# Two merge gates of a two-layer diffusion trunk as seven block products of summed operands

## The chip, the cores and the metric

One core of one Trainium2 chip runs the whole kernel. The metric is the device time of one execution in microseconds; the time before is the median of three runs.

## What is computed

Two layers work on 512 latent and 256 context positions of 1024 channels. A layer normalises and modulates its input to h, projects h to four mixers (A: dense attention, D: windowed attention with a sink, B: FNet mixing, C: gMLP gating), gates each mixer's output and merges the four:

```python
def _merge(h, outs, gates, w_br, w_merge, b_merge, w_out):
    yb = jnp.stack([o * jax.nn.silu(z) for o, z in zip(outs, gates)], axis=2)
    y = jnp.einsum('bnrw,rwd->bnrd', yb, w_br)
    g = jax.nn.sigmoid(h @ w_merge + b_merge).reshape(b, n, N_BRANCH, D_MODEL)
    return jnp.sum(g * y, axis=2) @ w_out
...
sh, sc, gt = _modulation(c, w_ada, b_ada)       # silu(c) @ w_ada + b_ada
h = _rms(x, norm_w) * (1.0 + sc[:, None, :]) + sh[:, None, :]
x = x + gt[:, None, :] * y
```

For every mixer r, h @ w_merge is a product of 768 x 1024 by 1024 x 1024 in layer 0 (latent and context together) and of 512 x 1024 in layer 1 (latent alone).

## The kernel before, in words

Activations lie channels first: a tile is 128 channels by 768 positions, columns 0 to 255 the context (NC), 256 to 767 the latents. h is eight such tiles, each as a rounded high part hh and a remainder hl; a weight tile (128 by 512, four 128 x 128 blocks) is likewise split into wh and wl, so that every product is three matmuls: wh with hh, wh with hl, wl with hh (mm3, lines 183 to 189; mmp, 191 to 197, runs over the blocks of a piece).

Weights come as a list of pieces in the order of use (`plan`, 138 to 153). wnext (175) takes the next one: it issues loads on SP's queue up to LOADS = 5 pieces ahead into three buffers (wload, line 161) and splits pieces up to two ahead of the one in use (wround: ScalarE casts wh on line 171, VectorE subtracts wl on line 172; three buffers each).

merge(r) (649 to 689) makes one mixer's share of the merged sum M. It loops over eight output tiles j: 8 blocks of 128 input channels by 3 matmuls, each for the 512 latent columns (bank gl) and the 256 context columns (gc); then the branch, 2 blocks by 3 matmuls for both widths (yl, and the other half of gc); then ScalarE's tanh of the gate (672), VectorE's product with the branch (674), and the sum into M, by a GpSimd DMA that adds (680), or on VectorE in the last pass (678), which also splits M into MH and ML (686, 687) for the output projection outp (964).

Layer 0 goes through it in this order: R_C, then R_A inside the filler, then R_D, then R_B. The attention generator (608 to 643: scores, maximum 577, exponential 585, transposes 601, products with v 634; one score bank, `s`) is driven against a filler of projections and merges (935): after each step the filler is advanced until its cost in ns has made up the pace, 4500 in layer 0 and 4000 in layer 1 (drive, 871). What the filler has left runs after the attention. R_D and R_B then run with a side generator under SIDE = 0.42: first fnet (785, the FNet's transforms, matmuls included, whose result is R_B's operand), then ada_rest (250): the column sums that make the remaining modulation rows, 24 rows of 128 in layer 0 (48 half rows by two vectors, c and c_ctx) and 8 in layer 1 (16 half rows, c alone). A half row is loaded on SP's queue (273) into one of three buffers it shares with the attention and multiplied and summed by VectorE (276). The costs and paces only set the order in which the program is written; a scheduler then orders each engine's instructions by that order and by when it reckons them ready and their buffers free.

Rope.finish (475) rotates q and k with tables cos and sin that are loaded once (408) and kept.

## Time and profile before

| | us |
|---|---|
| three runs | 1198.5, 1201.61, 1201.41 |
| their median | 1201.41 |
| the profiled execution | 1199.38 |
| its span, first to last instruction | 1197.5 |
| TensorE busy | 1176.4 (98%) |
| its weight loads | 1000.6 (84%) |
| VectorE busy | 734.6 (61%) |
| ScalarE busy | 471.9 (39%) |
| GpSimd busy | 14.4 (1%) |

The times of the profile are counted from the first instruction, so that its own execution is 1.9 us longer than its span. The granted clock of TensorE is 1.00 in every window. A busy share counts an instruction from its start to its end; the start of one matmul to the start of the next is shorter than a matmul's own duration, since they overlap, so the cost of a run of matmuls is read from starts.

### The profile page before, as it was taken

How to read it: one execution, taken by the hardware profiler on the slowest of the kernel's cores; microseconds unless marked ns; L12 is line 12 of the kernel's file. 1: busy time of each engine (PE TensorE's matmuls, PEld its weight loads, DVE VectorE, ACT ScalarE, POOL GpSimd, SP SyncE). 2: the span in 40 equal slices, each digit the busy share in tenths (PEclk: the TensorE clock that was granted, in tenths of full speed). 3: DMA queues.
4: the chain of work that ended last, by engine and by line, in shares of the span. 5: the costliest groups of instructions: out<-in, count | busy, mean ns of one | idle time of the engine just before them, and what ended most of it. 6: DMA issues, size and time to landing. Idle time of an engine off the chain costs nothing.

```text
span 1197.5 us, 18872 instructions
## 1 busy us (share of the span) xinstructions
PE 1176.4 (98%) x7164; PEld 1000.6 (84%) x7164; DVE 734.6 (61%) x1568; ACT 471.9 (39%) x935; POOL 14.4 (1%) x20
## 2 busy tenths in 40 slices
PE   6999999999999999999999999999999999999998
PEld 3789888888888888988888888887888888888887
DVE  5683567555555553577885468768656666476543
ACT  5443634333333332422333246545444343333431
POOL 0000000000000000000000000000000000000000
PEclk9999999999999999999999999999999999999999
DMA  8718114111112335567653454462322223355353
GB/s 305 247 34 203 55 38 104 49 45 49 54 49 54 75 84 121 128 182 201 183 167 103 132 166 139 136 178 81 100 67 75 63 65 91 99 169 155 97 171 124
DMA packets 76090, 138.81 MB, mean 116 GB/s; under 512 B 9056, under 2 KB 19424, under 8 KB 76000
## 3 DMA queue, kind: packets, MB, share of 16 engines
q1 hardware_dynamic: 66640, 120.30, 34.3%
q10 hardware_dynamic: 7056, 11.02, 3.1%
q0 software_dynamic: 2304, 6.29, 3.0%
q8 instruction: 56, 0.92, 0.3%
q14 instruction: 34, 0.28, 0.1%
HBM read 115.56 MB, written 4.19 MB: 100 GB/s over the span
## 4 chain that ended last, share of the span: by engine, by line
PE 93%; DMA 2%; DVE 2%; SPq 1%; ACT 1%; issue 0%; ACTq 0%
PE gl L186 10%; PE gl L187 10%; PE gl L189 10%; PE o L634 4%; PE tp L601 3%; PE gc L186 3%; PE gc L189 3%; PE gc L187 3%; PE ow L186 3%; PE ow L189 3%; PE ow L187 3%; PE p L186 3%; PE p L189 3%; PE p L187 3%; PE yl L186 2%; PE yl L187 2%
## 5 line engine op out<-in xcount | busy, mean ns | idle before, releaser
L171 ACT CAST wh<-wr 128x512 fp32r<-128x512 f32 (+1 forms) x320 | 184.6, 577 | 369.9 <-PE gc L187 95.7
L172 DVE TENSOR_TENSOR wl<-wr,wh 128x512 fp32r<-128x512 f32 (+1 forms) x320 | 203.2, 636 | 189.0 <-ACT wh L171 187.0
L186 PE MATMUL gl<-hh,wh 128*128 128x512 f32 x512 | 204.6, 400 | 0.0
L187 PE MATMUL gl<-hl,wh 128*128 128x512 f32 x512 | 200.5, 392 | 0.0
L189 PE MATMUL gl<-hh,wl 128*128 128x512 f32 x512 | 200.3, 391 | 0.0
L189 PEld LDWEIGHTS gl<-hh,wl 128*128 128x128 f32 x512 | 96.2, 188 | 20.8
L186 PEld LDWEIGHTS gl<-hh,wh 128*128 128x128 f32 x512 | 96.6, 189 | 16.6 <-ACT wh L171 0.2
L187 PEld LDWEIGHTS gl<-hl,wh 128*128 128x128 f32 x512 | 96.7, 189 | 16.2
L577 DVE TENSOR_REDUCE mx<-s 128x1 f32<-128x768 f32 (+3 forms) x80 | 61.6, 770 | 78.2 <-PE s L571 35.8
L585 ACT ACTIVATE p<-s,ng 128x768 f32<-128x768 f32 (+3 forms) x80 | 60.1, 751 | 102.6 <-DVE ng L582 58.5
L276 DVE CUSTOM_DVE_ANT_0 aj<-at,cb 128x512 f32<-128x512 f32 x112 | 72.7, 687 | 10.6 <-DMA at<-in_wadat_dram 10.6
L186 PE MATMUL gc<-hh,wh 128*128 128x256 f32 x256 | 73.6, 288 | 0.0
L189 PE MATMUL gc<-hh,wl 128*128 128x256 f32 x256 | 72.6, 283 | 0.0
L187 PE MATMUL gc<-hl,wh 128*128 128x256 f32 x256 | 72.5, 283 | 0.0
L186 PE MATMUL p<-hh,wh 128*128 128x512 f32 (+1 forms) x192 | 71.3, 371 | 0.0
L186 PE MATMUL ow<-MH,wh 128*128 128x512 f32 (+1 forms) x200 | 69.6, 348 | 1.0 <-DVE xn L976 1.0
L189 PE MATMUL ow<-MH,wl 128*128 128x512 f32 (+1 forms) x200 | 69.5, 348 | 0.8 <-DVE wl L172 0.8
L187 PE MATMUL ow<-ML,wh 128*128 128x512 f32 (+1 forms) x200 | 69.5, 348 | 0.0
L189 PE MATMUL p<-hh,wl 128*128 128x512 f32 (+1 forms) x192 | 68.3, 356 | 0.0
L187 PE MATMUL p<-hl,wh 128*128 128x512 f32 (+1 forms) x192 | 68.2, 355 | 0.0
L672 ACT ACTIVATE g<-gl,bmh 128x512 f32<-128x512 f32 x64 | 43.9, 686 | 56.2 <-PE gl L189 39.0
L601 PE MATMUL tp<-kconst,p 128*128 128x128 f32 x368 | 53.3, 273 | 0.0
(467 smaller groups left out, 2425.3 us busy)
## 6 DMA issues: line engine op xcount, KB each, us to landing
wr<-in_wm_dram SPq DMA_DIRECT2D x128, 256.0 KB, 2.7
wr<-in_win_dram SPq DMA_DIRECT2D x72, 256.0 KB, 2.8
at<-in_wadat_dram SPq DMA_DIRECT2D x64, 256.0 KB, 3.1
wr<-in_wo_dram SPq DMA_DIRECT2D x40, 256.0 KB, 2.9
aw<-in_wada_dram SPq DMA_DIRECT2D x16, 512.0 KB, 5.9
wr<-in_wm_dram SPq DMA_DIRECT2D x64, 128.0 KB, 2.2
ks<-yk SPq DMA_DIRECT2D x32, 192.0 KB, 4.2
M<-g POOLq DMA_DIRECT2D x16, 384.0 KB, 4.6
```

What stands on the lines that cost most here:

```text
L171: A.copy(hi[:, :n], raw[:, :n])
L172: V.tensor_sub(lo[:, :n], raw[:, :n], hi[:, :n].bitcast(F32))
L186: T.matmul(d, wh, xh[:, c0:c1], start=first and op, stop=False)
L187: T.matmul(d, wh, xl[:, c0:c1], start=False, stop=False)
L189: T.matmul(d, wl, xh[:, c0:c1], start=False, stop=last and cl)
L276: V.tensor_tensor_reduce(out=junk[:, :512], in0=w[:, :512], in1=cb[2 * v + half][:, :512], scale=0.5, scalar=0.0, op0=ALU.mult, op1=ALU.ad ...
L577: V.reduce_max(out=mx, in_=sv, axis=AX.X)
L585: A.activation(p[:, :nk], sv, AF.Exp, bias=ng, scale=0.125, accum_out=sm_)
L601: T.transpose(tp[:, (i - g0) * P:(i - g0 + 1) * P], p[:, i * P:(i + 1) * P], ident)
L634: T.matmul(dst[64 * hx:64 * hx + 64, :], vt[kt_ // 3][:, kt_ % 3, c0:c0 + 64], pts[hx][:, j * P:(j + 1) * P], start=(j == 0), stop=(j == l ...
L672: A.activation(g[:, q0:q1], gp, AF.Tanh, scale=0.5, bias=bmh[:, r * 8 + j:r * 8 + j + 1])
```

## The change

In layer 0 the gates of R_D and R_B are made by merge_s, for pairs of output tiles (j, j+4). The input channels are halved (tiles 0 to 3, 4 to 7), the positions are halved (H1 = 0 to 383, H2 = 384 to 767) and the outputs are halved (j, j+4), and the eight products of blocks become seven, of summed operands: combos sums the blocks of h once for both passes (into tiles T2, T3, T4 and T1; first_sum writes T1 over the right half of hh and hl 0 to 3), and a `prep` of four VectorE instructions a pair sums the weight tiles in place, ahead of the third block. A product is 4 blocks of channels by 3 matmuls of 384 columns. Bank z holds the first product, is copied out by ScalarE, and goes on accumulating; x and y hold two more, which VectorE adds to the copies. Four weight tiles of a pair come through the pool z, two rows of branch weights as before.

R_A's last three tiles (part 5 to 7) are held back from the filler, and the FNet and combos stand beside them; PACE of layer 0 is 3900 in place of 4500. ada_rest now goes through all half rows of the first half, then the second, with one row buffer of its own (the next load is written behind the sums of the last) and two buffers for c's rows, which it shares with the rotary tables; those are loaded anew for each use, on ScalarE's queue. Its steps are laced into R_C, z1, the FNet's projection and R_A, one for each 4800 of their cost, in both layers, and in layer 0 into R_D and R_B, one for each 6500. Layer 1's R_D and R_B keep the old form.

```diff
-PACE = (4500, 4000)
+PACE = (3900, 4000)
 STK = 1000
 WHOLE = 4
 LOADS, W_RAW, W_HI, W_LO = 5, 3, 3, 3
 SIDE = 0.42
+ADA, ADA_S = 4800, 6500
+HELD = 5
...
+        def merged_s(l, r):
+            def a(j, h):
+                return (wm[l, r, j, :, 512 * h:512 * h + 512], 512, "wraw" if h and j < 4 else "z")
+            def y(j):
+                return (wm[l, r, j, :, 1024:], 256)
+            first = [load(*a(0, 0)), load(*a(4, 0)), load(*a(4, 1)), load(*a(0, 1))]
...
+                def prep(a11=a11, a12=a12, a21=a21, a22=a22, s1=s1):
+                    t = tl("p", f"s1_{a11}")[:, :512]
+                    V.tensor_add(t, raws[a21], raws[a22])
+                    V.tensor_sub(raws[a21], raws[a11], raws[a21])
+                    V.tensor_sub(raws[a11], t, raws[a11])
+                    V.tensor_sub(raws[a12], raws[a12], raws[a11])
+                    s1.append(t)
+                item(a11, 512)
+                item(a12, 512)
+                item(a12, 512, prep, lambda k=a11: raws[k])
+                item(a12, 512, None, lambda k=a21: raws[k])
+                item(a12, 512, None, lambda s1=s1: s1[0])
+                item(y0, 256)
+                item(y0, 512, None, lambda k=a12: raws[k])
+                item(y0, 512, None, lambda k=a22: raws[k])
+                item(y1, 256)
...
+                src, n, tag = loads[k]
+                if tag == "z":
+                    raws[k] = tl("z", f"wr{k}")[:, :512]
+                else:
+                    raws[k] = pw.tile([P, 512], F32, name=f"wr{k}", tag="wraw", bufs=W_RAW)
+                nc.sync.dma_start(raws[k][:, :n], src)
...
+            wload(max(k for k, *_ in items[i:i + LOADS]))
+            wround(i + 2)
+            while prepped[0] < min(i + 3, len(items)):
+                prep = items[prepped[0]][2]
+                if prep:
+                    prep()
+                prepped[0] += 1
...
+            steps = [(half, l, j) for half in range(2) for l, j in names]
+            macc = {g: pc.tile([P, 8 if g else 16, 2, 2], F32, name=f"macc{g}{nv}", tag=f"macc{g}")
+                    for g in sorted({j // 16 for _, j in names})}
+            row, cb = [], []
+            def fetch(i):
+                if i < len(steps):
+                    half, l, j = steps[i]
+                    w = prow.tile([P, 512], F32, name=f"at{l}_{j}_{half}{nv}", tag="row")
+                    nc.sync.dma_start(w, wadat[l, j, :, half * 512:half * 512 + 512])
+                    row.append(w)
+            fetch(0)
...
+                for v in range(nv):
+                    junk = tl("sc", f"aj{l}_{j}_{half}{v}")
+                    V.tensor_tensor_reduce(
+                        out=junk[:, :512], in0=row[i], in1=cb[v], scale=0.5,
+                        scalar=0.0, op0=ALU.mult, op1=ALU.add, accum_out=macc[j // 16][:, j % 16, v, half:half + 1])
+                fetch(i + 1)
+                yield 1000
...
-        nc.sync.dma_start(rt_, krope)
...
+            def tables(name):
+                if not TAB:
+                    for i in range(2):
+                        t = prt.tile([P, NL], F32, name=f"rt{i}{name}", tag="rt")
+                        nc.scalar.dma_start(t, krope[:, i * NL:(i + 1) * NL])
+                        TAB.append(t)
+                return TAB
...
+            def combos():
+                t23 = [[[tl("k", f"T{n}{part}{i}{l}", F32R) for i in range(2)] for part in "hl"] for n in (2, 3)]
+                t4 = [pq.tile([P, 2, NT], F32R, name=f"T4{part}{l}", tag="q") for part in "hl"]
+                t1 = [tl("k", f"T1{i}{l}") for i in range(2)]
+                def at(ts, kk):
+                    return [t[kk // 2][:, (kk % 2) * HN:(kk % 2) * HN + HN] for t in ts]
+                for n in (11, 21, 22, 1, 2, 3, 4):
+                    BO[n] = []
+                for kk in range(4):
+                    fa, fb = tl("sc", f"fa{l}{kk}"), tl("p", f"fb{l}{kk}")
+                    for f, k_ in ((fa, kk), (fb, kk + 4)):
+                        V.tensor_add(f[:, WC], hh[k_][:, WC].bitcast(F32), hl[k_][:, WC].bitcast(F32))
+                    one = at([t1], kk)[0]
+                    V.tensor_sub(one, fa[:, H2], fa[:, H1])
+                    V.tensor_sub(fa[:, H2], fb[:, H2], fa[:, H2])
+                    V.tensor_sub(fb[:, H2], fb[:, H2], one)
+                    V.tensor_sub(fb[:, H1], fb[:, H1], fb[:, H2])
+                    two, three = at(t23[0], kk), at(t23[1], kk)
+                    four = [t[:, kk // 2, (kk % 2) * HN:(kk % 2) * HN + HN] for t in t4]
+                    for n, (hi, lo), src in ((2, two, fb[:, H2]), (3, three, fa[:, H2]), (4, four, fb[:, H1])):
+                        A.copy(hi, src)
+                        V.tensor_sub(lo, src, hi.bitcast(F32))
+                        BO[n].append((hi, lo))
+                    BO[1].append((one, None))
+                    BO[11].append((hh[kk][:, H1], hl[kk][:, H1]))
+                    BO[21].append((hh[kk + 4][:, H1], hl[kk + 4][:, H1]))
+                    BO[22].append((hh[kk + 4][:, H2], hl[kk + 4][:, H2]))
+                    yield 4000
...
+            def first_sum():
+                for kk in range(4):
+                    src, hi, lo = BO[1][kk][0], hh[kk][:, H2], hl[kk][:, H2]
+                    A.copy(hi, src)
+                    V.tensor_sub(lo, src, hi.bitcast(F32))
+                    BO[1][kk] = (hi, lo)
+            def block(dst, n, start):
+                wh, wl = wnext()
+                for i, (xh, xl) in enumerate(BO[n]):
+                    q = slice(i * P, (i + 1) * P)
+                    T.matmul(dst, wh[:, q], xh, start=start and i == 0, stop=False, skip_group_check=True)
+                    T.matmul(dst, wh[:, q], xl, start=False, stop=False, skip_group_check=True)
+                    T.matmul(dst, wl[:, q], xh, start=False, stop=i == 3, skip_group_check=True)
+                    yield 1.27 * HN
+            def branch(r, j, tags):
+                y_l = bank(f"yl{l}{r}{j}", tags[0])
+                yd = [(y_l, NC, NT, True, True)]
+                if not last:
+                    yd.append((bank(f"yc{l}{r}{j}", tags[1])[:, :NC], 0, NC, True, True))
+                wh, wl = wnext()
+                yield from mmp(yd, wh, wl, YB[r], 0, 2)
+                return yd
+            def merge_s(r, final=False):
+                for j in range(4):
+                    z, x, y = (bank(f"{n}{l}{r}{j}")[:, :HN] for n in "zxy")
+                    g0, g1 = (tl("sc", f"g{l}{r}{i}") for i in (j, j + 4))
+                    bias = [bmh[:, r * 8 + i:r * 8 + i + 1] for i in (j, j + 4)]
+                    def gate(i, jj, g, yd):
+                        for yp, q0, q1, _, _ in reversed(yd):
+                            V.scalar_tensor_tensor(out=g[:, q0:q1], in0=g[:, q0:q1], scalar=1.0, in1=yp,
+                                                   op0=ALU.add, op1=ALU.mult)
+                        if final:
+                            V.tensor_add(M[jj][:, WC], M[jj][:, WC], g[:, WC])
+                        else:
+                            G.dma_start(M[jj], g, accum_op=ALU.add)
+                    yield from block(z, 11, True)
+                    A.copy(g0[:, H1], z)
+                    yield from block(x, 21, True)
+                    V.tensor_add(g0[:, H1], x, g0[:, H1])
+                    A.activation(g0[:, H1], g0[:, H1], AF.Tanh, scale=0.5, bias=bias[0])
+                    yield from block(z, 2, False)
+                    A.copy(g1[:, H1], z)
+                    yield from block(y, 3, True)
+                    yield from block(z, 1, False)
+                    A.copy(g1[:, H2], z)
+                    V.tensor_add(g1[:, H2], y, g1[:, H2])
+                    yd = yield from branch(r, j, ("o", "t"))
+                    yield from block(z, 22, False)
+                    A.activation(g0[:, H2], z, AF.Tanh, scale=0.5, bias=bias[0])
+                    gate(0, j, g0, yd)
+                    yield from block(y, 4, False)
+                    V.tensor_add(g1[:, H1], y, g1[:, H1])
+                    A.activation(g1[:, WC], g1[:, WC], AF.Tanh, scale=0.5, bias=bias[1])
+                    yd = yield from branch(r, j + 4, ("t", "o"))
+                    gate(1, j + 4, g1, yd)
...
+            def laced(main, other, per):
+                bal = 0
+                for x in main:
+                    yield x
+                    bal += x or 0
+                    if bal >= per:
+                        bal -= per
+                        next(other, None)
...
-                ("mc", lambda: merge(R_C, first=True)), ("z1", lambda: zblock(1)),
-                ("b", bproj), ("ma", ("a0", lambda: merge(R_A))),
+                ("mc", lambda: laced(merge(R_C, first=True), ada, ADA)), ("z1", lambda: laced(zblock(1), ada, ADA)),
+                ("b", lambda: laced(bproj(), ada, ADA)),
+                ("ma", ("a0", lambda: laced(merge(R_A, part=range(own)), ada, ADA))),
...
-            if not last:
-                adas = [(0, j) for j in range(16, 24)] + [(1, j) for j in range(16)]
-                side = seq([("fnet", fnet), ("ada", lambda: ada_rest(adas))])
+            if l == 0:
+                side = seq([("fnet", fnet), ("sums", combos)])
+                drive(paced(merge(R_A, ctag="o", part=range(own, KT)), 1.0), side)
+                run(side)
+                first_sum()
+                run(laced(merge_s(R_D), ada, ADA_S))
+                run(laced(merge_s(R_B, final=True), ada, ADA_S))
+                side = ada
             else:
-                side = seq([("fnet", fnet), ("ada", lambda: ada_rest([(1, j) for j in range(16, 24)], 1))])
-            drive(paced(merge(R_D, ctag="o"), SIDE), side)
-            while "fnet" not in flags:
-                next(side)
-            drive(paced(merge(R_B, final=True, ctag="o"), SIDE), side)
+                side = seq([("fnet", fnet), ("ada", lambda: ada)])
+                drive(paced(merge(R_D, ctag="o"), SIDE), side)
+                while "fnet" not in flags:
+                    next(side)
+                drive(paced(merge(R_B, final=True, ctag="o"), SIDE), side)
...
-            xn = [tl("yb", f"xn{i}") for i in range(KT)]
+            xn = [tl("yb" if i < 4 else "z", f"xn{i}") for i in range(KT)]
```

## Rows read from the trace of the kernel before

**Rows 1.** The page: busy time of the engines, and the chain by engine.

```profile
PE 1176.4 (98%) x7164; PEld 1000.6 (84%) x7164; DVE 734.6 (61%) x1568; ACT 471.9 (39%) x935; POOL 14.4 (1%) x20
...
PE 93%; DMA 2%; DVE 2%; SPq 1%; ACT 1%; issue 0%; ACTq 0%
```

**Rows 2.** TensorE's waits: who waited for whom, us in all, times, longest.

```profile
PE n L314 <- DVE sq L312: 8.1, 4, 7.2
...
PE s L557 <- ACT p L585: 1.0, 1, 1.0
```

**Rows 3.** Windows: length, then busy us and instructions of PE, PEld, DVE, ACT, POOL.

```profile
200.00:290.00 90.00, 90.00 (x611) 77.75 (x611) 46.34 (x105) 32.45 (x70) 0.00 (x0) 1.00 0.24 64
...
449.00:473.00 24.00, 24.00 (x141) 21.28 (x142) 8.04 (x14) 6.78 (x12) 1.72 (x2) 1.00 0.43 104
...
473.11:504.00 30.89, 30.89 (x198) 27.92 (x197) 16.09 (x49) 10.43 (x20) 1.72 (x2) 1.00 0.51 128
...
562.00:647.70 85.70, 85.70 (x493) 75.58 (x493) 70.96 (x177) 28.13 (x48) 0.86 (x1) 1.00 0.50 149
...
810.00:920.00 110.00, 110.00 (x680) 89.91 (x679) 74.33 (x146) 52.40 (x105) 0.00 (x0) 1.00 0.28 77
```

**Rows 4.** TensorE in time, R_D's start to outp: start, us, line, operation.

```profile
473.11 0.40 PE L186 MATMUL gl<-hh,wh 128*128 128x512 f32 x1
...
574.51 0.40 PE L186 MATMUL gl<-hh,wh 128*128 128x512 f32 x1
...
577.26 0.28 PE L186 MATMUL gc<-hh,wh 128*128 128x256 f32 x1
...
578.69 0.40 PE L186 MATMUL gl<-hh,wh 128*128 128x512 f32 x1
...
582.87 0.40 PE L186 MATMUL yl<-yb300h,wh 128*128 128x512 f32 x1
...
584.97 0.40 PE L186 MATMUL gl<-hh,wh 128*128 128x512 f32 x1
...
647.73 0.40 PE L186 MATMUL ow<-MH,wh 128*128 128x512 f32 x1
```

**Rows 5.** TensorE in time: a score of 384 columns in attention D.

```profile
305.82 0.34 PE L570 MATMUL s<-ks,qs 128*128 128x384 f32 x1
...
306.00 0.34 PE L571 MATMUL s<-ks,qs 128*128 128x384 f32 x1
```

**Rows 6.** VectorE in time, in R_B.

```profile
575.79 0.42 DVE L172 TENSOR_TENSOR wl<-wr,wh 128x256 fp32r<-128x256 f32 x1
...
576.12 0.95 DVE L678 TENSOR_TENSOR M<-M,g 128x768 f32<-128x768 f32 x1
...
576.99 0.69 DVE L276 CUSTOM_DVE_ANT_0 aj<-at,cb 128x512 f32<-128x512 f32 x1
...
577.60 0.69 DVE L276 CUSTOM_DVE_ANT_0 aj<-at,cb 128x512 f32<-128x512 f32 x1
```

**Rows 7.** Groups by form, ScalarE: count, busy us, mean ns, idle before.

```profile
L171 ACT CAST wh<-wr 128x512 fp32r<-128x512 f32 x256 | 158.6, 620 | 315.8 <-PE gl L187 89.4 <-PE gc L187 59.3 <-issue 45.7
...
L171 ACT CAST wh<-wr 128x256 fp32r<-128x256 f32 x64 | 26.0, 407 | 54.1 <-PE gc L187 36.4 <-PE p L187 4.8 <-issue 3.6
...
L686 ACT ACTIVATE MH<-M 128x768 fp32r<-128x768 f32 x8 | 6.8, 847 | 13.3 <-DVE M L678 13.3
```

**Rows 8.** The FNet's table kd: durations, first and last start in us.

```profile
L795 PE MATMUL gcs<-wf,kd x8: 270/275/348, 476.1 to 1039.1; 128*128 128x128 f32 x8
...
L788 ACTq DMA_DIRECT2D kd<-in_kdft_dram x2: 334/348/361, 446.0 to 1008.1; - x2
```

**Rows 9.** All engines in time: one exponential and the next score in its bank.

```profile
248.58 0.90 ACT L585 ACTIVATE p<-s,ng 128x768 f32<-128x768 f32 x1
...
252.65 0.28 PE L557 MATMUL s<-ks,qs 128*128 128x256 f32 x1
```

**Rows 10.** SP's queue: its row loads' waits.

```profile
SPq L273 <- DVE macc L276: 46.0, 55, 1.7
```

More of the change, by code (lines that the diff above doesn't have):

```diff
@@ L126, in hybrid_trunk, with load, item, pieces @@
         cnt = [0]
+        loads, raws, items = [], {}, []
+        def load(src, n, tag="wraw"):
+            loads.append((src, n, tag))
+            return len(loads) - 1
+        def item(k, n, prep=None, get=None):
+            items.append((k + 1, n, prep, get or (lambda: raws[k][:, :n])))
+        def pieces(ps):
+            for src, n in ps:
+                item(load(src, n), n)
         def blocks(l, *bs):
-            return [(win[l, b, :, h * 512:h * 512 + 512], 512) for b in bs for h in range(2)]
+            pieces([(win[l, b, :, h * 512:h * 512 + 512], 512) for b in bs for h in range(2)])
@@ L135, in outw @@
         def outw(l, j0=0):
[L136 to L138 removed]
+            pieces([(wo[l, j, :, h * 512:h * 512 + 512], 512) for j in range(j0, KT) for h in range(2)])
         for l in range(DEPTH):
             if l == 0:
[L141 removed]
+                blocks(l, B_V0, B_V1)
             else:
[L143 to L150 removed]
+                pieces(2 * [(wkv[kk], 512) for kk in range(KT)])
+                blocks(l, B_QA1, B_QA2)
@@ L151, in hybrid_trunk @@
+            blocks(l, B_CU, B_CU + 1, B_CV0, B_CV1, B_CZ, B_CZ + 1, B_QD1, B_QD2, B_AZ, B_AZ + 1)
+            merged(l, R_C)
+            blocks(l, B_DZ, B_DZ + 1, B_BF, B_BF + 1, B_BZ, B_BZ + 1)
+            merged(l, R_A)
+            for r in (R_D, R_B):
+                (merged if l else merged_s)(l, r)
+            outw(l)
             if l == 0:
-                both[0] = len(plan)
-                plan += outw(l, WHOLE)
-        loaded, ready = [], []
+                outw(l, WHOLE)
+        ready, prepped, TAB = [], [0], []
```

110 lines of the change are left out of this document (54 added, 56 removed).

## The prediction

> **What bounds the kernel now.** I read the busy line and the chain first [rows 1]: TensorE is busy for 98% of the span and makes 93% of the chain that ended last. TensorE's own waits come next [rows 2]: the longest is 8.1 us while the first norm is made, and scores that wait for an exponential come to 1.0 us in all. The windows [rows 3] say the same by stage: in the attention of layer 0 (200 to 290 us), behind it (449 to 473), beside the FNet (473 to 504), in the R_B pass (562 to 648) and in layer 1's attention TensorE is busy for the whole window at a granted clock of 1.00, that is 2.4 GHz, while VectorE is busy for 51%, 34%, 52%, 83% and 68% of it. So the time falls by what leaves TensorE's queue, and rises by what makes it wait; VectorE is the engine that can make it wait, in R_B above all.
>
> **What leaves TensorE.** TensorE in time [rows 4] prices the old tile: twelve 512-wide matmuls from 574.51 to 577.26 (0.229 us each), twelve 256-wide from 577.26 to 578.69 (0.119 each), a gate of one tile from 574.51 to 582.87 (8.36 us) and a whole tile, gate and branch, to 584.97 (10.46 us, so the branch is 2.10). R_D and R_B run from 473.11 to 647.73: 174.6 us, which is 16 tiles of 10.46 (167.4) and 7.3 us of FNet matmuls between them.
>
> The new gate of a pair of tiles (j, j+4) is seven blocks of 12 matmuls of 384 columns, 84 in place of 96 of each width. No 3-pass 384-wide gate is in the trace. Half way between the two widths above lies 0.174 us; the nearest row, a lone 384-wide score matmul, took 0.18 from its start to the next [rows 5]. I take 0.174, since the scores stand between other widths and the blocks will follow each other; 0.18 stays as the other end. Then a pair costs 84 x 0.174 = 14.62 us in place of 2 x 8.36 = 16.72: 2.10 us less, and over 8 pairs (two passes of four) **16.8 us less**. At 0.18 it is 1.60 a pair and 12.8 in all. The branches keep their matmuls, the FNet's only move. The Trainium skill (TensorE: Matmul & The Clock Gate, section "Back-to-back issue gap") gives N/2.4 + 2.5 ns between matmuls, so 215.8, 109.2 and 162.5 ns for the three widths; by it the saving would be an estimated 15.6 us, and this trace's matmuls are each some 10 ns slower than that. The same section has 131 ns for sustained 512-wide matmuls; by that the trace disagrees (229).
>
> **What comes to VectorE, in the two passes.** From start to start VectorE takes 0.33 us for 256 columns, 0.61 for 512 and 0.87 for 768 [rows 6]; 384 is taken half way, 0.47. A pair in R_D: nine low halves of weights (7 x 0.61 + 2 x 0.33 = 4.93; three 512-wide ones more than two old tiles have), four sums of weight tiles (2.44), three additions of partial products (1.41), four gate products (1.88): 10.7 us, where two old tiles took 5.0. R_B adds the sums into M and the splits, 4 x 0.87, as before: 14.1. The column sums (a step is two of 0.61) come on top. The program's own costs place them: at one step for 4800 of cost, R_C (78.0 us of cost), z1 (15.6), the FNet's projection with its z (31.2) and R_A's five tiles (48.8) hold 16, 3, 6 and 10 resumptions, 35 of 53; at 6500, R_D's 70.2 us hold ten, and the last eight fall in R_B's first three pairs. A pair's 17.56 us of cost is 2.7 steps, 3.3 us. So VectorE carries 14.0 of the pair's 18.8 us in R_D and 17.4, or 93%, in R_B's first three pairs, against 83% before. ScalarE has three more casts and three copies a pair: 3 x 0.62 and three between 0.41 and 0.62 [rows 7], some 3.4 us on an engine that was 33% busy there [rows 3]. Both engines' additions are off the path as long as they fit in the pair.
>
> Cover for each wait inside a pair: a weight tile's cast and low half (0.62 and 0.69) start when the block two before begins, so they have 4.2 us; the four sums before the third block add 2.4 and still fit. I price what does not fit at **2 us lost** over both passes and the held tiles: zero would be the rows of the old R_B, where VectorE at 83% cost TensorE nothing, and 10 us is the far end (the first rival).
>
> **The held-back tiles.** Tiles 5 to 7 of R_A (31.4 us) and the FNet (7.3) are 38.7 us of TensorE. VectorE has 3 x 2.5 for the tiles, some 10 for the FNet (16.1 busy in 473 to 504 [rows 3], less twelve instructions of tiles) and 4 x (2 x 0.87 + 7 x 0.47) = 20.1 for the summed operands: 38 us. That is full, but it need not all lie there: instructions do run ahead of their place when their buffers are free. The FNet's table kd was fetched at 446.0, 30 us before its matmul at 476.1, and before R_D, beside which it is written, began [rows 8]. In front of the held tiles lies a stretch in which VectorE was 34% busy (449 to 473). Overwriting the right half of hh (four casts, four differences, 2 us) has the first four blocks, 8 us, as cover. Price: nothing beyond the 2 us above. If the sums come late, the third block of R_D waits once.
>
> **Attention of layer 0.** The pace falls from 4500 to 3900: 49 paces less 600 are 29.4 us of cost, and the three tiles held back are 29.3 of cost, so the filler still outlasts the attention by as much. Per unit the next scores come 0.64 us earlier. They need the score bank, whose exponential ended at 249.48, 3.17 us before the scores at 252.65 [rows 9]; 2.5 us are left, and a step of column sums with one weight tile in front of the maximum takes 1.22 + 0.61. VectorE rises from 51% to some 80%. Layer 1 runs at a pace of 4000 with VectorE at 68% and loses nothing [rows 3], and gets one 0.61 us sum every 5 us. I take zero; the far end is a quarter of 48 units losing 1 us, 12 us.
>
> **Edits that cost nothing.** The row loads, 64 as before, stay on SP's queue, but now beside attention: written behind the copies that stack q and k, they pass only weight loads. Each waits for VectorE's sums (before, 46.0 us in 55 waits, the longest 1.7 us [rows 10]); a weight load queued behind one waits as long, and it is asked for five pieces ahead, over 10 us. The rotary tables move to ScalarE's queue, where c's rows were, in buffers that are free long before their use. If that cover were gone, a late weight load would show as a wait for wh.
>
> **Sum.** -16.8 + 2 = -14.8 us against this execution's own 1199.4 (span 1197.5): 1184.6. The median of the three runs is 1201.4, 2.0 above it, so I forecast **1186.6** for the median.
>
> **Rivals.**
> *VectorE becomes the bound in R_B, or the summed operands are late.* For it: 93% with in-order waits, and 38 us of work in 38.7. If each of R_B's first three pairs grows to 21 us (6.6 lost) and R_D's third block waits 3, the gain is 7: **1194**. Against: work runs ahead [rows 8], and the column sums are the work that can wait.
> *The open bank z is emptied late (slower).* Three times a pair z is read out by ScalarE and then written on, and y once after an addition: 32 re-entries. The cover is one block, 2.09 us, for a copy of some 0.5; but ScalarE works in order, and a cast of a summed weight tile in front of it waits for VectorE's four sums (2.44), or an MH of 0.85 [rows 7] stands there. It costs TensorE from the point where a copy ends 2.1 us after its block. At 0.53 us a re-entry the whole gain is gone; 2.44 + 0.62 + 0.5 less 2.09 is 1.5 for the one behind the sums, and if the others lose 0.5, a pair loses 3.0 and the passes 24: **1209**. Against: the order of the old kernel lets ready work pass, and its tanh on gl cost TensorE nothing in R_B [rows 3]. The Trainium skill (Perfetto Trace Analysis, section "Matmuls") advises that independent groups rotate through different PSUM banks so that emptying one overlaps the next; here the same bank is opened again, with one block of another bank between. By that rule the cover is what decides, and no run here shows it yet.
> *Attention waits at the new pace.* 12 us lost: **1198 to 1199**, no change. Against: layer 1.
> *All of it, and no stall:* **1184.6**, or 1182 where the run is as far below the median as the lowest was (1198.5).
> *The seven blocks save nothing:* if 384 columns cost what 512 do, 84 x 0.229 = 19.2 a pair, 20 us slower; the 0.18 row is against it, and I fold it into the slower case.
>
> **Chances.** Forecast 0.55; full gain 0.10; VectorE 0.20; attention 0.08; z, or the width, 0.07. 0.3%, or 3.6 us, is about what a measurement of this kernel can tell from no change, so faster means under 1197.8 and slower over 1205.0: faster 0.85 (the first three cases), same 0.08, slower 0.07. The range 1181.5 to 1197 takes in the full gain, 0.18 us a matmul (1190.6) and the VectorE rival, and leaves out attention and z.
>
> **What would show it.** Right: block matmuls 0.174 us apart; a pair in 18.8 us; R_D's first block to the output projection's first matmul in 150.6 us in place of 174.6; no TensorE wait over 1 us in that stretch; attention windows at full TensorE. Wrong: waits of z's matmuls for ScalarE's copies, of TensorE for wl or for the T tiles at R_D's third block, of scores for the exponential; or blocks at 0.18 or more.

## The result, and the profile after

The change made the kernel slower: 1206.11 us median of 6 runs (1204.19 to 1209.09) against 1198.92 of 6 runs of the kernel before, ratio 1.0059 (95% interval 1.0041 to 1.0077). The forecast was 1186.6, the range 1181.5 to 1197: both were missed, and the sign too.

The page of the changed kernel, for [rows 1]. TensorE is busy 6.8 us less, but in a span 6.9 us longer (1204.4); VectorE has 59.5 us more, and its share of the chain went from 2% to 5%:

```profile
PE 1169.6 (97%) x7068; PEld 999.9 (83%) x7068; DVE 794.1 (66%) x1688; ACT 499.6 (41%) x991; POOL 14.1 (1%) x20
...
PE 88%; DVE 5%; DMA 3%; ACT 2%; issue 1%; SPq 1%; ACTq 0%; DVEq 0%
```

TensorE's waits (us in all, times, longest), for [rows 2]. The new ones are z, gl and gc; those of scores rose from 1.0 to 2.7. The view counts idle time from the modelled end of the matmul before; a wait in the text is counted from starts and is 0.15 to 0.2 us longer (3.8 for the 3.6 here):

```profile
...
PE z L815 <- ACT wh L226: 5.5, 2, 3.6
PE s L631 <- ACT p L659: 2.7, 4, 1.0
PE gl L250 <- DVE wl L227: 1.7, 1, 1.7
...
PE z L815 <- ACT g L845: 1.4, 1, 1.4
PE gc L247 <- DVE g L748: 1.4, 1, 1.4
```

Windows of the changed kernel, columns as in [rows 3]. TensorE falls short beside the held-back tiles (460 to 500: 33.73 of 40, VectorE 38.49), and behind the longest wait the granted clock drops to 0.67:

```profile
200.00:290.00 90.00, 89.32 (x597) 75.44 (x595) 62.16 (x159) 32.82 (x72) 0.00 (x0) 1.00 0.33 93
...
460.00:500.00 40.00, 33.73 (x199) 29.55 (x197) 38.49 (x87) 18.33 (x38) 2.58 (x3) 1.00 0.36 86
...
500.00:504.00 4.00, 3.49 (x12) 3.17 (x13) 2.28 (x4) 1.40 (x3) 0.00 (x0) 0.67 0.39 131
504.00:508.00 4.00, 4.00 (x22) 4.00 (x21) 3.50 (x9) 1.43 (x3) 0.00 (x0) 0.90 0.22 66
...
580.00:620.00 40.00, 38.23 (x217) 36.23 (x216) 34.38 (x69) 18.50 (x34) 0.00 (x0) 1.00 0.31 94
...
810.00:920.00 110.00, 109.26 (x672) 88.90 (x671) 81.05 (x163) 51.15 (x99) 0.00 (x0) 1.00 0.37 105
```

TensorE in time, for [rows 4]: R_D's first, second and third block, the second and third pair, the output projection:

```profile
492.45 0.34 PE L815 MATMUL z<-hh,wh 128*128 128x384 f32 x1
...
494.54 0.33 PE L815 MATMUL x<-hh,wh 128*128 128x384 f32 x1
...
500.40 0.44 PE L815 MATMUL z<-T2h,wh 128*128 128x384 f32 x1 [3.62 <-ACT wh L226]
...
501.74 0.52 PE L816 MATMUL z<-T2l,wh 128*128 128x384 f32 x1
...
517.07 0.34 PE L815 MATMUL z<-hh,wh 128*128 128x384 f32 x1
...
535.87 0.34 PE L815 MATMUL z<-hh,wh 128*128 128x384 f32 x1
...
653.72 0.39 PE L247 MATMUL ow<-MH,wh 128*128 128x512 f32 x1
```

The first block's twelve matmuls take 2.09 us, 0.174 each, and the second pair 18.80 us: the width was priced exactly. But the first pair took 24.62, and the whole from R_D to the output projection 161.3 where eight clean pairs would be 150.4. VectorE in time shows why the third block came late: splits of the FNet's result, then four instructions that overwrite hl's right half (one row, x4), stand in front of the four sums of weight tiles (the first and the last here) that the block's cast needs:

```profile
494.14 0.96 DVE L263 TENSOR_TENSOR yb310l<-yf,yb310h 128x768 fp32r<-128x768 f32 x1
...
495.35 1.96 DVE L808 TENSOR_TENSOR hl<-T,hh 128x384 fp32r<-128x384 f32 x4
497.23 0.68 DVE L173 TENSOR_TENSOR s<-wr,wr 128x512 f32<-128x512 f32 x1
...
499.74 0.69 DVE L176 TENSOR_TENSOR wr<-wr,wr 128x512 f32<-128x512 f32 x1
```

**The 6.9 us of the two spans**, from marks of the two traces: before the first score +1.1; beside the held-back tiles two waits of 1.9 and 1.5, +3.4; R_D's first pair +5.8 (a wait of 3.8 and 2.0 behind it, slower matmuls for the most part); R_B's waits +5.1 (0.9, 1.7 and 2.5 over 18.80 in its first, second and fourth pair); behind the output projection's start +0.9; the blocks -17.0 (eight pairs of 18.80 in place of 20.92); what is left, +7.6, lies between the first score and the FNet. Idle time of TensorE makes up only 2.8 of it (six waits, 3.8 us, against 1.0 before); the rest stands in no wait of the view. That stretch holds waits like this one (all engines, rows of the weight loads and of other lines left out): a column sum stands between a context unit's maximum and its negation, the exponential follows, and the next score waits for it:

```profile
272.06 0.41 DVE L651 TENSOR_REDUCE mx<-s 128x1 f32<-128x256 f32 x1
...
272.39 0.68 DVE L342 CUSTOM_DVE_ANT_0 aj<-at,cb 128x512 f32<-128x512 f32 x1
...
272.99 0.15 DVE L654 TENSOR_SCALAR ng<-mx 128x1 f32<-128x1 f32 x1
...
273.51 0.47 ACT L659 ACTIVATE p<-s,ng 128x256 f32<-128x256 f32 x1
...
274.12 0.38 PE L631 MATMUL s<-ks,qs 128*128 128x256 f32 x1 [0.66 <-ACT p L659]
```

### The profile page after: what moved, and what is told of

Same layout as the page of the kernel before. It is cut to its first block, busy times and chain, and to the rows that moved or that the text cites. A ratio compares the mean times of both kernels' runs of the same rounds, so it can differ in the third digit from the quotient of the medians.

```text
span 1204.4 us, 18892 instructions
## 1 busy us (share of the span) xinstructions
PE 1169.6 (97%) x7068; PEld 999.9 (83%) x7068; DVE 794.1 (66%) x1688; ACT 499.6 (41%) x991; POOL 14.1 (1%) x20
## 4 chain that ended last, share of the span: by engine, by line
PE 88%; DVE 5%; DMA 3%; ACT 2%; issue 1%; SPq 1%; ACTq 0%; DVEq 0%
PE gl L247 7%; PE gl L250 7%; PE gl L248 7%; PE o L708 4%; PE tp L675 3%; PE ow L247 3%; PE ow L248 3%; PE ow L250 3%; PE p L247 3%; PE p L248 3%; PE p L250 3%; PE yl L250 2%; PE yl L247 2%; PE yl L248 2%; PE z L815 2%; PE z L817 2%
## 5 line engine op out<-in xcount | busy, mean ns | idle before, releaser
L247 PE MATMUL gl<-hh,wh 128*128 128x512 f32 x384 | 154.1, 401 | 0.0
L250 PE MATMUL gl<-hh,wl 128*128 128x512 f32 x384 | 150.3, 391 | 1.7 <-DVE wl L227 1.7
L248 PE MATMUL gl<-hl,wh 128*128 128x512 f32 x384 | 149.9, 390 | 0.0
L250 PEld LDWEIGHTS gl<-hh,wl 128*128 128x128 f32 x384 | 72.1, 188 | 17.9 <-DVE wl L227 2.1
L247 PEld LDWEIGHTS gl<-hh,wh 128*128 128x128 f32 x384 | 72.3, 188 | 12.9 <-ACT g L746 0.2
L248 PEld LDWEIGHTS gl<-hl,wh 128*128 128x128 f32 x384 | 72.4, 189 | 12.6
L708 PEld LDWEIGHTS o<-pt,vt 128*64 128x64 f32 x736 | 40.8, 136 | 16.8 <-issue 13.7
L675 PEld LDWEIGHTS tp<-kconst,p 128*128 128x128 f32 x368 | 44.6, 140 | 11.0 <-issue 0.9
L708 PE MATMUL o<-pt,vt 128*64 128x128 f32 x736 | 52.4, 279 | 0.6 <-DVE pt L677 0.6
L677 DVE COPY pt<-tp 128x384 f32<-128x384 f32 (+1 forms) x80 | 41.9, 524 | 8.9 <-PE tp L675 8.9
```

The costliest lines, as they stand in the source:

```text
L247: T.matmul(d, wh, xh[:, c0:c1], start=first and op, stop=False)
L248: T.matmul(d, wh, xl[:, c0:c1], start=False, stop=False)
L250: T.matmul(d, wl, xh[:, c0:c1], start=False, stop=last and cl)
L675: T.transpose(tp[:, (i - g0) * P:(i - g0 + 1) * P], p[:, i * P:(i + 1) * P], ident)
L677: V.tensor_copy(pt[:, g0 * P:g1 * P], tp[:, :(g1 - g0) * P])
L708: T.matmul(dst[64 * hx:64 * hx + 64, :], vt[kt_ // 3][:, kt_ % 3, c0:c0 + 64], pts[hx][:, j * P:(j + 1) * P], start=(j == 0), stop=(j == l ...
```

## The experiments

Theory 1: VectorE has no room beside the held-back tiles. Theory 2: the moved column sums are in the way. Theory 3: the pace, or holding tiles back, costs the attention. Diffs are against the changed kernel unless said; ratios are to the kernel before, where the changed kernel stands at 1.0059.

**e1, more cover.**
```diff
-HELD = 5
+HELD = 3
```


> Five tiles of R_A held back in place of three, nothing else changed; TensorE's cover for the FNet and the summed operands grows by 19.5 us. Theory 1 (VectorE is full beside the held-back tiles, so the summed operands come late): the 3.8 us wait at R_D's third block, the two waits of 1.9 and 1.5 us beside the held tiles and the low clock behind them (1.7 us) go; about 8 us less than the changed kernel, ratio to the kernel before 0.998 to 1.000. Theory 2 (the moved column sums are what delays scores and weight tiles): the same waits in attention and in R_B, ratio 1.004 to 1.006. Theory 3 (holding tiles back starves the attention): TensorE loses more before 450 us, ratio over 1.008.

1.0114 (1.0099 to 1.0128): theory 1 fails in this form. With five tiles beside them the FNet and the sums of h's blocks were still written ahead of most of the tiles, and VectorE was full there, not over the stretch (its windows):

```profile
452.00:458.00 6.00, 6.00 (x37) 5.34 (x36) 6.00 (x15) 1.94 (x5) 0.86 (x1) 1.00 0.30 87
464.00:470.00 6.00, 3.02 (x12) 2.17 (x12) 6.00 (x12) 2.65 (x6) 0.00 (x0) 1.00 0.15 45
470.00:476.00 6.00, 5.37 (x28) 5.22 (x29) 5.19 (x12) 2.67 (x6) 0.86 (x1) 0.72 0.46 86
```

The third block waited 3.3 us all the same. Of the 7.4 us between this trace and the changed kernel's, 4.4 lie between the last score and R_D, in the stretch of these windows. Theory 3's starved attention was not it either, though the ratio lies in its band: from its first to its last score it took 311.5 us, against 312.5 in the changed kernel.

**e2, no column sums.**
```diff
-                ada = ada_rest([(0, j) for j in range(16, 24)] + [(1, j) for j in range(16)])
+                ada = iter(())
```


> Leaves out the column sums of the modulation rows and their row loads (the rows are set to 0.5); everything else as in the changed kernel. Theory 1: the third block's wait and the waits beside the held tiles stay nearly as they are (no sums stand there but the one by R_A's tiles), only R_B's two waits of 1.6 and 2.1 us shrink; ratio 1.001 to 1.003. Theory 2: the attention's lost 5 us, R_B's 4 and half of R_D's come back; ratio 0.996 to 0.999.

1.0028 (1.0017 to 1.0039), in theory 1's band: the waits of 1.9, 1.5 and 3.8 us stayed to the hundredth, R_B's of 0.5 and 1.6 went; that of 2.0 at its last pair, which was to shrink, stayed. From the first score to the FNet's first matmul it took 337.7 us against 341.3: the sums cost the attention 3.6 of its 7.6, which is theory 2's part (it forecast 5).

**e3, the old gates with all other edits.**
```diff
-                (merged if l else merged_s)(l, r)
+                merged(l, r)
...
-                run(laced(merge_s(R_D), ada, ADA_S))
+                run(laced(merge(R_D, ctag="o"), ada, ADA_S))
```


> The moved column sums, the pace of 3900 and the held-back tiles of the changed kernel, with the old two gates of layer 0 (no summed operands, no summed weights). The block products alone took 16.8 us out; what they cost beside held tiles and in the passes is 10.7 + 3.4 by the two traces. Theory 1: this kernel is 16.8 - 14 = 3 us above the changed one or level with it, ratio 1.006 to 1.009, its loss all before 450 us. Theory 2: as the sums also delay the old gates, 1.010 or more, with waits in R_D or R_B. If the losses before 450 us come from the summed operands, 1.000 to 1.002.

1.0082 (1.0069 to 1.0095), in theory 1's band. From the first score to the output projection the same matmuls as before took 545.4 us in place of 537.0, and R_D and R_B had no wait: what the edits around the blocks cost lies ahead of them, 8.4 us.

**e4, plain blocks of h.**
```diff
-                side = seq([("fnet", fnet), ("sums", combos)])
+                side = seq([("fnet", fnet)])
...
-                first_sum()
+                for n, k0, h_ in ((11, 0, H1), (21, 4, H1), (22, 4, H2), (1, 0, H2), (2, 0, H1), (3, 4, H1), (4, 4, H2)):
+                    BO[n] = [(hh[k0 + i][:, h_], hl[k0 + i][:, h_]) for i in range(4)]
```


> The seven block products with plain blocks of h in place of the summed ones: leaves out the sums of h's blocks and the overwriting of hh and hl; the weights are still summed, the matmuls are as many. Theory 1: waits beside the held tiles and at the third block all but go, the clock stays at 1.00; 8 to 9 us less than the changed kernel, ratio 0.998 to 0.999. Theory 2: at most 3 us less, ratio 1.003 to 1.005. If the third block's wait is the weights' sums alone (four additions behind other VectorE work), it stays at 2 us or more.

1.0042 (1.0028 to 1.0057), a miss for theory 1: the waits beside the held tiles went, that of the third block stayed at 3.5 us, so VectorE's load was not its only cause. SP's queue, ScalarE and VectorE of this run: the FNet's result is cast when R_A's last branch is done, the weight loads of R_D's first pair start when the first of the two result tiles has been split, and the weights' sums wait for the load:

```profile
489.68 0.83 ACT L262 CAST yb300h<-yf 128x768 fp32r<-128x768 f32 x1 [1.12 <-PE gc L248]
...
490.55 0.96 DVE L263 TENSOR_TENSOR yb300l<-yf,yb300h 128x768 fp32r<-128x768 f32 x1 [0.41 <-ACT yb300h L262]
...
491.54 1.53 SPq L216 DMA_DIRECT2D wr<-in_wm_dram  x2
...
494.41 0.69 DVE L173 TENSOR_TENSOR s<-wr,wr 128x512 f32<-128x512 f32 x1 [1.70 <-DMA wr<-in_wm_dram]
```

**e5, the third load from another pool.**
```diff
-                return (..., "wraw" if h and j < 4 else "z")
+                return (..., "wraw" if h and j < 4 else "p" if h and j == 4 and r == R_D else "z")
```


> One weight tile of R_D's first pair (the third of the four that are loaded for its sums) goes into the pool p in place of z; nothing else. The run without the summed operands kept the wait at R_D's third block (3.4 us), and there the sums of the weights began when a load landed that was issued 0.1 us after the FNet's result was split. Theory 4 (a chain of buffers: R_A's operands hold the pool yb until the last held-back tile, so the FNet's result cannot be split, so two of the four z buffers stay taken, so the third load and all behind it on SP's queue are late): the third block's wait falls from 3.8 us to under 0.5 and the clock stays at 1.00 behind it; 4 to 5.5 us less than the changed kernel, ratio 1.001 to 1.003. Theory 1 (VectorE is full there): the wait stays at 3 us or more, 1.005 to 1.007.

1.0075 (1.0063 to 1.0088), a miss for theory 4: the load that the changed kernel issued at 490.66 went out at 484.97, and the block waited 3.8 us as before, now for VectorE's order alone, as in the changed kernel:

```profile
494.38 0.95 DVE L263 TENSOR_TENSOR yb300l<-yf,yb300h 128x768 fp32r<-128x768 f32 x1
...
496.46 1.96 DVE L808 TENSOR_TENSOR hl<-T,hh 128x384 fp32r<-128x384 f32 x4
498.33 0.68 DVE L173 TENSOR_TENSOR s<-wr,wr 128x512 f32<-128x512 f32 x1
```

**e6, the pace; e7, the sums spread; e8, the column sums in R_D.**
```diff
-PACE = (3900, 4000)
+PACE = (4500, 4000)
```


> Layer 0's pace back at 4500, all else as in the changed kernel. The run without column sums kept 3.6 of the 7.2 us that TensorE loses from 110 us to the FNet. If that is the pace (theory 3): the extra wait of the first units (120 to 134 us, 2.8 us in place of 1.2) goes, and the whole comes 3 us lower, 1.003 to 1.004, unless the filler runs out before the attention does (the last units then wait, 5 us more). If it is the tables or the order of the sums: as the changed kernel, 1.005 to 1.007.

1.0033 (1.0021 to 1.0044), as theory 3 has it for the pace: 3.1 us less.

```diff
-                drive(paced(merge(R_A, ctag="o", part=range(own, KT)), 1.0), side)
+                drive(paced(merge(R_A, ctag="o", part=range(own, KT)), 0.75), side)
```


> Beside the held-back tiles the side generator is advanced at 0.75 of their cost in place of 1.0, so that the sums of h's blocks are written over all three tiles and not ahead of the last. Theory 1 in its narrow form (the sums stand in front of a weight tile's low half and of a product of the gate, 1.9 and 1.5 us): these two waits fall to under 1 us together, 2.5 us less than the changed kernel, ratio 1.003 to 1.005; the third block's wait stays. If VectorE simply has no room there: the same 3.4 us at other places, 1.005 to 1.007.

1.0069 (1.0057 to 1.0082), the rival: no wait beside the held tiles, and 1.3 and 6.3 us in R_D's first blocks. The work only moved.

```diff
-ADA, ADA_S = 4800, 6500
+ADA, ADA_S = 4800, 3800
```


> In the two passes a step of column sums for each 3800 of cost in place of 6500, so that the last 18 are written within R_D and none in R_B. Theory 2: R_B's waits of 0.5 and 1.6 us go, as in the run without sums, that of 2.1 at its last pair stays; 2 us less if R_D takes the sums without a wait, ratio 1.003 to 1.005. If VectorE is full in R_D with them (14 + 2 of 18.8 us a pair): waits in R_D in their place, 1.006 or more.

1.0106 (1.0092 to 1.0120), the rival: R_B lost its two waits, R_D got six of 0.3 to 1.5 us behind its first pair, and 4.4 at the third block. R_D has no room for twice the sums.

**e9, both chains of the third block cut** (e4 and e5 together).


> Both edits at R_D's third block at once: plain blocks of h in place of the summed ones (leaves out the sums of h's blocks and the overwriting of hh and hl), and the third load of the first pair in pool p. Each alone left the wait at 3.5 to 3.8 us: without the sums a load ended last, with the early load VectorE's work did (splits of the FNet's result and the overwriting, until 498.3 us, in front of the weights' sums). Theory 5 (two chains of nearly the same length end there, and either one alone holds the block): the wait falls below 0.5 us; 4 to 5 us less than without the sums alone, ratio 1.000 to 1.001. Rival: a third thing holds it (the four sums themselves, 2.9 us from first to last, begin too late in any case): the wait stays over 2 us, 1.003 to 1.005.

1.0013 (1.0004 to 1.0022), 0.03% above the band; the wait is gone, the three blocks start 2.09 and 2.08 us apart:

```profile
490.14 0.34 PE L815 MATMUL z<-hh,wh 128*128 128x384 f32 x1
...
492.23 0.33 PE L815 MATMUL x<-hh,wh 128*128 128x384 f32 x1
...
494.31 0.34 PE L815 MATMUL z<-hh,wh 128*128 128x384 f32 x1
```

So theory 5 is shown: a late load and VectorE's work each hold that block for 3.5 us or more. (e4 leaves out the sums of h's blocks and the overwriting together; these two are not told apart.)

**e10 to e12, column sums beside the output projection.** e10 has that alone; e11 adds pace 4500, e5's load, spread 0.75 and the overwriting behind the second block; e12 has four tiles held back, spread 0.56 and pace 4300 in place of e11's three, 0.75 and 4500.
```diff
-            steps = [(half, l, j) for half in range(2) for l, j in names]
+            steps = [(half, l, j) for m in (0, 1) for half in range(2) for l, j in names if l == m]
...
-                run(laced(merge_s(R_B, final=True), ada, ADA_S))
+                run(merge_s(R_B, final=True))
```


> The column sums go through layer 0's rows first, then layer 1's, and none are laced into R_B; what is left of layer 1's rows runs beside the output projection, where VectorE was 45% busy. Theory 2: R_B's waits of 0.5 and 1.6 us go, that of 2.1 stays; 2 us less than the changed kernel, ratio 1.003 to 1.005. If the rows' sums then hold the next layer's norm or the projection's end: 1.006 or more, with the loss behind 650 us.

> Pace 4500, the early load, the side generator at 0.75, the overwriting of hh and hl written behind the second block, and the sums out of R_B, together. If the causes add up: 3 (pace) + 2 (R_B) + 2 (VectorE's order at the third block) less than the changed kernel, ratio 0.999 to 1.001. VectorE has some 44 us of work up to the third block against 41 us of TensorE's, so that at least 3 us of waits should stay there; if they stay at 6 or more, 1.002 to 1.003.

> As the kernel with all five edits, but with four tiles held back (10.4 us more of TensorE beside the sums), the side generator at 0.56, and the pace at 4300 so that the filler still lasts. If the room for VectorE is what is missing (theory 1), the waits beside the held tiles and at the third block fall below 2 us in all: ratio 0.995 to 0.998, faster than both kernels. If holding tiles back costs as much as it gives (the run with five held back was 6 us slower than the changed kernel), 1.001 or more.

1.0193 (1.0174 to 1.0212), 1.0162 (1.0143 to 1.0181) and 1.0133 (1.0118 to 1.0149). e10's rival had it (1.006 or more, lost behind 650 us); e11 and e12, which are built on e10, missed. The output projection up to layer 1's first matmul took 15 to 21 us more than the changed kernel's 69.9. There the sums follow each other, and with one row buffer each waits for its own load, some 4 us a step. They stand in VectorE's queue ahead of the last sums into x (L1184 in e12), which free the projection's banks; TensorE waited for those 11.8 us at once (VectorE in time, e12):

```profile
691.81 0.69 DVE L342 CUSTOM_DVE_ANT_0 aj<-at,cb 128x512 f32<-128x512 f32 x1 [2.16 <-DMA at<-in_wadat_dram]
...
696.88 0.69 DVE L342 CUSTOM_DVE_ANT_0 aj<-at,cb 128x512 f32<-128x512 f32 x1 [2.82 <-DMA at<-in_wadat_dram]
...
698.11 0.48 DVE L1184 SCALAR_TENSOR_TENSOR xn<-ow,mod,xr 128x256 f32<-128x256 f32 x1
```

In e11, with three tiles held back, R_D's first pair took 30.0 us, with waits of 3.0 and 4.0 us in it: the early load, the spread and the late overwriting do not free the block there. But e12's R_D and R_B took 154.3 us, without a wait beside the held tiles or at the third block.

**e13 to e15, room with the column sums back.** e13 is e12 with the steps and R_B's lacing of the changed kernel; e14 also has ADA 3900; e15 has only the lines of PACE, HELD and drive. e5's load, in e13 and e14, is not printed again.
```diff
-PACE = (3900, 4000)
+PACE = (4300, 4000)
...
-HELD = 5
+HELD = 4
...
+                    if r == R_D and j == 0:
+                        first_sum()
                     yield from block(z, 2, False)
...
-                drive(paced(merge(R_A, ctag="o", part=range(own, KT)), 1.0), side)
+                drive(paced(merge(R_A, ctag="o", part=range(own, KT)), 0.56), side)
                 run(side)
-                first_sum()
```


> Four tiles held back, side generator at 0.56, pace 4300, the early load and the late overwriting, with the column sums as in the changed kernel. In the run before with these edits the stretch from R_D's first block to the output projection took 154.3 us with the sums gone from R_B. Theory 5 (room for VectorE and two chains): 155 to 157 us there, attention 2 us over the kernel before; ratio to the kernel before 0.994 to 0.998. If the sums in R_D and R_B were what held the blocks (theory 2): 160 us or more there, ratio 1.000 to 1.004.

0.9982 (0.9973 to 0.9991): faster than before, 0.02% above the band; 156.7 us from R_D to the projection.

> The same with a step of column sums for each 3900 of cost in place of 4800 ahead of R_D, so that all but one or two are done before R_B. R_B's waits of 0.5 and 1.6 us should go; 7 steps more stand in the attention's stretch, where 35 steps cost 3.6 us, so 0.7 more there. Theory 5: 1 to 2 us less than the other, 0.993 to 0.997. If the sums in attention cost a wait for each one that meets a context unit: level with it or above, to 0.999.

0.9980 (0.9971 to 0.9990): level with e13. R_B's waits for column sums went and three waits came in the attention, as the rival has it.

> Four tiles held back, side generator at 0.56, pace 4300 alone; the third load stays in pool z and the overwriting ahead of R_D. Theory 5: the waits beside the held tiles go, the third block waits for its load, 3 to 4 us, with the low clock behind it; 4 to 5 us above the run with all edits, ratio 0.999 to 1.002. If room is all that was missing: level with that run.

1.0020 (1.0011 to 1.0029): no wait beside the held tiles, 3.4 us at the third block, where VectorE itself stood idle until the load had landed:

```profile
490.93 0.69 DVE L173 TENSOR_TENSOR s<-wr,wr 128x512 f32<-128x512 f32 x1 [1.46 <-DMA wr<-in_wm_dram]
```

Room for VectorE and the late load are separate causes: e15 has the room without the early load, e5 and e11 the early load without the room, and all three wait. What the late overwriting gives beside these two was not tested by itself.

**e17, the kernel before with pace 3900** (read by its ratio alone).
```diff
-PACE = (4500, 4000)
+PACE = (3900, 4000)
```


> The kernel before with layer 0's pace at 3900 in place of 4500, nothing else. Theory 3 (the pace alone costs the attention): more waits of scores and of products with v in the first units, 110 to 135 us, and 3 to 4 us in all: ratio 1.002 to 1.004. If the pace only costs beside the moved column sums: 0.999 to 1.001.

1.0023 (1.0014 to 1.0032): the pace alone costs 2.8 us, column sums or not.

**e16 and e18, the last pair's sum tile** (on e14; e18 with ADA 4300).
```diff
-                    t = tl("p", f"s1_{a11}")[:, :512]
+                    t = tl("z" if r == R_B and j == 3 else "p", f"s1_{a11}")[:, :512]
```


> The run with room, both third-block edits and earlier column sums, and the sum tile of R_B's last pair taken from pool z in place of p. Theory 6 (that tile queues behind the two tiles that the split of M takes from p): the wait of 2.0 us at R_B's last pair goes, the R_B pass takes 4 x 18.8 = 75.2 us; 2 us less than that run, ratio 0.995 to 0.997. If VectorE has no time there: the wait stays, 0.997 to 0.999.

In e14 the sums of the last pair stand behind the last addition into M (VectorE in time):

```profile
624.75 0.96 DVE L840 TENSOR_TENSOR M<-M,g 128x768 f32<-128x768 f32 x1
625.63 0.68 DVE L173 TENSOR_TENSOR s<-wr,wr 128x512 f32<-128x512 f32 x1
...
629.49 1.29 DVE L227 TENSOR_TENSOR wl<-wr,wh 128x512 fp32r<-128x512 f32 x2
```

With the tile from z they went ahead of it, and the wait of 2.0 us went with the slow matmuls behind it (the last pair took 18.80 us in place of e14's 22.76): 0.9944 (0.9930 to 0.9959), 1192.75 us, below the band and the best of all, 1.1% under the changed kernel (0.9944 / 1.0059). R_D's first block starts at 491.58 and the projection at 641.96; windows of e16 beside the held tiles, over R_D and over R_B:

```profile
460.00:500.00 40.00, 40.00 (x235) 36.39 (x234) 38.59 (x79) 19.77 (x41) 3.44 (x4) 1.00 0.50 123
491.58:566.80 75.22, 75.22 (x435) 73.11 (x434) 61.31 (x133) 34.97 (x63) 6.88 (x8) 1.00 0.59 154
566.80:641.96 75.16, 75.16 (x434) 73.04 (x434) 53.55 (x92) 37.32 (x67) 0.86 (x1) 1.00 0.28 78
```

> The same with a step of column sums for each 4300 of cost ahead of R_D in place of 3900, so that some four steps fall in R_B. The sums cost 3.9 us more in attention at 3900 than at 4800 and 3.9 less in R_B, by the two traces. If each place has a free share: 1 us less than at 3900. If the waits come one by one as sums meet a context unit or a weight tile: level, 0.995 to 0.998.

0.9947 (0.9934 to 0.9960): level with e16. Its trace has two waits in R_B again and 3.8 us less in the attention.

## Why the prediction was wrong

**Right: the width and the pair.** 0.174 us a matmul, 18.80 us a pair. Without a stall R_D and R_B take 150.4 us in e16, forecast 150.6, so the saving of 16.8 is real. By the formula for an isolated matmul in the Trainium skill (TensorE: Matmul & The Clock Gate, section "Back-to-back issue gap") this width would take an estimated 162.5 ns; the trace has 174 and decides.

**Right but for one wait: the re-opened bank z.** In e16 no block waits although z is written on three times a pair: one block of another bank, 2.09 us, was cover enough. In the changed kernel the rival's own chain came once, in R_B's second pair, for 1.6 us (it had priced 1.5). VectorE, without a pause since a column sum whose row came late, reached the addition into M late, and ScalarE's copy of z stood behind the MH that waited for it and behind the cast of a sum:

```profile
587.40 0.69 DVE L342 CUSTOM_DVE_ANT_0 aj<-at,cb 128x512 f32<-128x512 f32 x1 [1.75 <-DMA at<-in_wadat_dram]
...
597.48 0.84 ACT L870 ACTIVATE MH<-M 128x768 fp32r<-128x768 f32 x1 [1.52 <-DVE M L840]
598.23 0.60 ACT L226 CAST wh<-s 128x512 fp32r<-128x512 f32 x1
598.74 0.47 ACT L845 COPY g<-z 128x384 f32<-128x384 f32 x1
```

In e2 and e16 the copy stands ahead of that MH. The Trainium skill's advice that independent groups rotate through different banks (Perfetto Trace Analysis, section "Matmuls") is not contradicted by these runs.

**Wrong: "Price: nothing beyond the 2 us above" for the held-back tiles.** The step took it that the summed operands would run ahead of their place into a stretch with an idle VectorE, as the FNet's table had. They did not: single additions of h's parts ran from 454.6 us on, but the first cast of T2 was at 472.3 us, 19 us behind the FNet's first matmul, though VectorE was busy for only 9.0 of the 20 us from 440 to 460. What held the rest was not traced. Price: 3.4 beside the tiles and 5.8 in the first pair. "If the sums come late, the third block of R_D waits once" named the place, but the price of the rival, 3 us, left out the low clock behind it, and the cause was not the sums alone: a second chain (yb held by R_A's operands, z by the FNet's unsplit result, weight loads behind it on SP) was nowhere in the prediction. The count of free buffers was not made for the held-back order.

**Wrong: "I take zero" for the attention of layer 0.** It lost 7.6 us: 3.6 by the column sums (e2), 2.8 to 3.1 by the pace (e17, e6), the rest unassigned. VectorE was busy for 69% of the window from 200 to 290 us, less than the forecast 80%; the wait shown above came from where a sum stood, not from a full engine. Layer 1, the reason given for zero, has one sum a step in place of two. The far end, 12 us, held it. This is also why the best run falls short of the forecast: from the first score to the output projection e16 takes 528.3 us against 537.0 before, 8.7 less, though its blocks take off 17.0 and nothing waits from the held tiles on; some 8.3 us are still lost ahead of them.

**Mis-sized: "2 us lost" over both passes and the held tiles.** They lost 14.3 us: the 9.2 above and 5.1 in R_B. There 0.9 and 1.7 went where column sums stood in front of the addition that reads y and of the addition into M (both gone in e2 and e14), 2.5 at the last pair, whose sum tile queued behind the split of M in pool p (e16). That the row loads cost nothing was wrong here too: the first of these began with VectorE's own wait for a late row, 1.75 us.

**Wrong: rivals taken one at a time.** Late operands (1194) and the attention (1198) have different places and different causes: e2 and e6 shorten the attention and leave the third block's wait. Both came, together with R_B's waits; their losses add, and the sum goes over the kernel before. The chance of that stood nowhere: slower had 0.07, for z or the width alone.

Open: the 1.1 us ahead of the first score was not traced to a cause; it is within the scatter there, since the same matmul starts between 84.8 and 87.9 us in traces of the changed kernel and its variants. Nor was the part of the attention's loss traced that is no idle time. A larger pool yb was not tried.

## What to carry to other kernels

When work is held back to cover other work, list for every pool what the held work keeps alive, and follow each tile that then cannot be freed to the load that wants its buffer: here two pools and a load queue in a row led to one late block. Whether an engine has room is not told by its busy share: VectorE was busy 38.5 of 40 us beside the held tiles in the changed kernel and 38.6 in the best one, where TensorE lost nothing; what counts is what stands in front of the instruction that the bottleneck needs. And where several cheap edits each have a rival, add the rivals up before giving a chance to "faster".

## What the runs showed of the hardware that was not expected

Behind the 3.8 us wait TensorE's granted clock was 0.67 over 4 us and 0.90 over the next 4, means of the two levels, 2.4 and 1.2 GHz. Ten matmuls in a row there took 0.52 us in place of 0.33 and started 0.32 us apart, at the lower level: with a short wait for a low half, 2.0 us on top of the wait. Behind the wait of 2.0 us at R_B's last pair the window from 620 to 660 us showed 1.00 in the changed kernel and 0.96 in e2:

```profile
620.00:660.00 40.00, 38.09 (x215) 35.48 (x214) 29.56 (x55) 18.42 (x32) 0.00 (x0) 1.00 0.33 105
620.00:660.00 40.00, 38.15 (x205) 35.23 (x204) 26.05 (x44) 16.81 (x29) 0.00 (x0) 0.96 0.25 76
```

So the same wait had two prices: the last pair took 2.5 us over 18.80 in the changed kernel and 4.0 in e2 and in e14. What decided it was not tested.

In e16's pairs 384-wide matmuls start 0.173 to 0.174 us apart, whether the next one goes to the same bank or to another.
